# The linear recurrence of a two-layer model, computed in two stages by way of DRAM

## The chip, the cores and the metric

The kernel runs on one core of a Trainium2 chip. The metric is the device time of one execution in microseconds. Three executions of the kernel before took 2215.34, 2216.55 and 2222.05 us, median 2216.55.

## The reference

A model of two layers and one more block, 512 tokens of width 1024, all float32. The change lies in the first layer, the RWKV-7 time mix, with 32 heads of 64 features:

```python
r = xr @ w_in[0]; k = xk @ w_in[1]; v = xv @ w_in[2]; g = xg @ w_in[3]      # 1024 -> 2048 each
w_log = -softplus(-(w0 + tanh(xw @ w1) @ w2)) - 0.5
decay = exp(-exp(w_log));  a = sigmoid(a0 + (xa @ a1) @ a2)
kk = heads(k * k_k);  kk = kk / max(norm(kk), L2_EPS)
k = k * (1 + (a - 1) * k_a)
# per head and token t, state S of 64 x 64:
#   S = S * decay_t - (S kk_t)(a_t * kk_t)^T + v_t k_t^T ;  y_t = S r_t
y = head_group_norm(y, lnx_w, lnx_b)
bonus = sum(r * k * r_k, per head) * v
y = (y + bonus) * silu(g)
out = y @ w_out
```

Behind it come a short convolution layer and a block with attention, a long depthwise convolution and a gated feed-forward part. The change doesn't touch those.

## The kernel before

A float32 product of full width is made of three products in a rounded format: high x high, high x low, low x high ("dense" work; a k-group is one 128-row slice of the contraction, three matmuls of 128x512). The low part of a weight is the weight less its rounded copy. The products of the recurrence are plain float32.

`pre_phase` normalises, makes the token-shifted inputs and the value projection (to DRAM, `vD`). `scan_phase` then does everything up to the gate. It goes over 16 pairs of heads `j`. For one pair it makes the low-rank parts of decay and a (L617, L618), the k and r projections (16 k-groups, L701 to L703), and on VectorE the scaled keys `KB` and the vectors `ZR`. The tokens are cut into 8 chunks of 64. For all chunks of the pair, `gram` (L837) makes the 128x128 products of `KB` and `ZR`, which are masked (L845); `N` (L870) is the strictly triangular part, whose inverse `X` is found by 31 steps of one multiply and one subtract on VectorE (L923, L931) for the 32x32 diagonal blocks, and by two rounds of small products (L975) for the rest.

Then the 8 chunks follow one another. In each, TensorE makes `wy` from masked gram blocks and values (L1024) and from the state (L1033); ScalarE copies it, negated, to `Wn` (L1041); TensorE multiplies by the inverse (`U`, L1055); VectorE scales and copies `U` beside the values (L1063); TensorE makes the state's increment (`Sp`, L1072) and VectorE adds it to the decayed state (L1083, L1081 in the first chunk). The outputs get their last term from L1092. Each pair ends in a group norm: mean (L1160), 8 squared sums on ScalarE (L1168), a power on GpSimd (L1176), 8 scalings on ScalarE, then gain, bias, a transpose (L1197), and a store to `yD`.

After the pairs come 16 gate tiles: 8 k-groups each (L1283 to L1285), silu (L1291) into an SBUF tile, and a multiply by the stored y (L1299). `post_phase` begins with the output projection, for which `prep` splits those tiles in two parts.

The order of instructions on all five engines in this stage is written out by a planner, `list_schedule`. It takes the operations with their costs, priorities, dependences and buffer counts and, on a model of the engines, always starts the earliest one. In its model TensorE costs twice as much when too little work came shortly before, and a dense k-group is moved ahead when the recent share of work falls below `DENSITY`. Projections run `LAG` = 3 pairs ahead of the recurrence, and `pace` ties them to its links.

Of the kernel before, what the change touches and what calls it, by code (L numbers as in the profile page):

```python
# [25 lines left out]
C = 64  # L26
# [126 lines left out]
def two_block_kernel(ctx, tc, A, out):  # L153
# [100 lines left out]
    yD = dram.tile([DI, T], F32, tag="yD", name="yD")  # L254

    with ExitStack() as rk_ctx:
        hid = rk_ctx.enter_context(tc.tile_pool(name="hid", bufs=1))
        pd = rk_ctx.enter_context(tc.tile_pool(name="pd", bufs=2, space=PSUM))
        sgs, sconst, ahead = [], {}, {}
# [24 lines left out]
def pre_phase(nc, tc, A, E):  # L284
# [3 lines left out]
    vD, xgD, sconst, ahead = (E[k] for k in ("vD", "xgD", "sconst", "ahead"))  # L288

    def ht(shape, name, dt=F32):  # L290
        return hid.tile(shape, dt, tag=name, name=name)

    hidw, hida = ht([P, T], "hidw", F32R), ht([P, T], "hida", F32R)
    with ExitStack() as s:
# [213 lines left out]
        pack("pkB", ["b_conv_branch_2", "conv_dw_b_2", "conv_ln_g_2", "conv_ln_b_2"], hp, ps8, ahead["sp"])  # L508
# [7 lines left out]
        gmask = sconst["gmask"] = ht([P, 2 * P], "gmask")  # L516
        for b in (0, 64):
            for i in range(4):
                op = ALU.is_gt if i in (1, 2) else ALU.is_ge
                nc.gpsimd.affine_select(out=gmask[b:b + 64, 64 * i:64 * i + 64], in_=ones[b:b + 64, 0:64],  # L520
                                        pattern=[[1, 64]], compare_op=op, fill=0.0, base=0, channel_multiplier=-1)
        reset = sconst["reset"] = ht([P, NC, C + 1], "reset")
        nc.gpsimd.memset(reset, 1.0)
        nc.gpsimd.memset(reset[:, :, 0:1], 0.0)
        hind = sconst["hind"] = ht([P, 2], "hind")
        nc.gpsimd.memset(hind, 0.0)
        nc.gpsimd.memset(hind[0:64, 0:1], 1.0)
        nc.gpsimd.memset(hind[64:128, 1:2], 1.0)
# [9 lines left out]
        xone = sconst["xone"] = ht([P, 8, 32], "xone")  # L538
# [14 lines left out]
def scan_phase(nc, tc, A, E):  # L553
    col, cols, ident, ones, mhalf = (E[k] for k in ("col", "cols", "ident", "ones", "mhalf"))
    xr, xk, vD, xgD, yD, rc = (E[k] for k in ("xr", "xk", "vD", "xgD", "yD", "rc"))
    hidw, hida, wraw, whl, pd, kept = (E[k] for k in ("hidw", "hida", "wraw", "whl", "pd", "hid"))
    heads = [slice(0, 64), slice(64, 128)]
    with ExitStack() as s:
        sc = s.enter_context(tc.tile_pool(name="sc", bufs=1))
        pm = s.enter_context(tc.tile_pool(name="pm", bufs=3, space=PSUM))  # L560
        pc = s.enter_context(tc.tile_pool(name="pc", bufs=1, space=PSUM))

        def st(shape, name, bufs=1, dt=F32):
            return sc.tile(shape, dt, tag=name, name=name, bufs=bufs)
# [23 lines left out]
        def done_ahead():  # L588
            pass
# [7 lines left out]
        def build(j):  # L597
# [8 lines left out]
            if j == 0:  # L606
                S.update(E["ahead"])
# [1348 lines left out]
```

## Time and profile before

| | |
|---|---|
| median of three runs | 2216.55 us |
| profiled execution | 2209.47 us |
| its span, first to last instruction | 2207.8 us |
| PE / DVE / ACT / POOL busy in the span | 94 / 53 / 41 / 37 % |
| mean granted TensorE clock | 0.967 of full |
| HBM read / written | 175.80 / 14.68 MB |

PE is TensorE, DVE VectorE, ACT ScalarE, POOL GpSimd, SP SyncE (it issues the transfers). "L701" is line 701 of the kernel. Durations of PE instructions overlap in a pipeline, so the distance from one start to the next tells what one costs, not its duration. A float32 product of the recurrence appears in the timeline as two instructions (x4 stands for two products). "PEclk" is the granted clock as a share of the full one. In brackets stands how long an engine was idle before an instruction and what released it.

### The profile page before, as it was taken

To read this page: it belongs to the slowest core of one execution; us is meant where nothing else is said; L and a number is where in the kernel's file an instruction comes from. 1 tells how busy PE (TensorE), PEld (TensorE's weight loads), DVE (VectorE), ACT (ScalarE), POOL (GpSimd) and SP (SyncE) were. 2 spreads that over 40 slices of the span, in tenths; PEclk is the share of its full clock that TensorE was granted. 3 is DMA by queue.
4 is the path that set the end of the run, shared out by engine and by line. 5 is a ranking of instruction groups with operands and counts; after the bars stand their busy time and mean duration, and the time that the engine had idled before them with its cause. 6 is when DMAs were issued, how large, how long until landed. Compare 5 with 4: busy or idle time off the path is not lost.

```text
span 2207.8 us, 33093 instructions
## 1 busy us (share of the span) xinstructions
PE 2076.1 (94%) x12644; PEld 1600.6 (72%) x12644; DVE 1172.2 (53%) x2758; ACT 895.2 (41%) x1829; POOL 818.3 (37%) x710
## 2 busy tenths in 40 slices
PE   7998889889988999999999999999699999999998
PEld 5776666666666667788888888787466788888886
DVE  7959898888988762223333321379654253111101
ACT  5433465565555454323222222333476443222221
POOL 4220010110011233636555554665233366544442
PEclk9989999989898999999999999999799999999999
DMA  4341121121213233423333333333111242333321
GB/s 157 111 131 56 39 61 57 49 68 40 62 53 94 80 90 112 162 77 105 96 96 95 96 96 115 104 107 95 38 39 53 78 137 86 96 96 96 105 96 67
DMA packets 271607, 192.63 MB, mean 87 GB/s; under 512 B 12696, under 2 KB 238296, under 8 KB 271448
## 3 DMA queue, kind: packets, MB, share of 16 engines
q1 hardware_dynamic: 271448, 190.51, 28.4%
q8 instruction: 99, 1.62, 0.3%
q14 instruction: 60, 0.49, 0.1%
HBM read 175.80 MB, written 14.68 MB: 86 GB/s over the span
## 4 chain that ended last, share of the span: by engine, by line
PE 73%; DVE 16%; ACT 5%; issue 3%; POOL 2%; DMA 2%; SPq 0%; DVEq 0%; POOLq 0%; ACTq 0%
PE b L86 11%; PE b L85 11%; PE b L87 11%; PE b L120 5%; PE b L121 5%; PE b L119 5%; DVE conv L1730 4%; PE ps_d L701 3%; PE ps_d L703 2%; PE ps_d L702 2%; PE U L1055 2%; PE ps_g L1283 2%; DVE xtmp L923 2%; DVE X L931 1%; PE wy L1033 1%
## 5 line engine op out<-in xcount | busy, mean ns | idle before, releaser
L73 POOL TENSOR_TENSOR wl<-wr,wh 128x512 fp32r<-128x512 f32 (+1 forms) x463 | 639.8, 1404 | 602.2 <-ACT wh L65 596.2
L65 ACT CAST wh<-wr 128x1024 fp32r<-128x1024 f32 (+1 forms) x241 | 245.4, 1020 | 721.6 <-PE b L86 463.5
L87 PE MATMUL b<-s,wl 128*128 128x512 f32 x1024 | 404.7, 395 | 0.0
L86 PE MATMUL b<-s,wh 128*128 128x512 f32 x1024 | 404.4, 395 | 0.0
L85 PE MATMUL b<-s,wh 128*128 128x512 f32 x1024 | 403.4, 394 | 0.0
L85 PEld LDWEIGHTS b<-s,wh 128*128 128x128 f32 x1024 | 192.8, 188 | 47.2 <-issue 1.5
L86 PEld LDWEIGHTS b<-s,wh 128*128 128x128 f32 x1024 | 192.9, 188 | 46.0 <-issue 1.4
L87 PEld LDWEIGHTS b<-s,wl 128*128 128x128 f32 x1024 | 193.0, 188 | 43.6 <-issue 0.8
L1730 DVE SCALAR_TENSOR_TENSOR conv<-up,pkC,conv 128x512 f32<-128x512 f32 x120 | 117.0, 1040 | 0.4
L120 PE MATMUL b<-wl,s 128*128 128x512 f32 x288 | 113.9, 395 | 1.1 <-POOL wl L73 1.1
L923 DVE TENSOR_TENSOR xtmp<-dn,X 128x60 f32<-128x60 f32 (+24 forms) x496 | 109.1, 220 | 9.0
L119 PE MATMUL b<-wh,s 128*128 128x512 f32 x288 | 111.9, 396 | 1.2 <-ACT s L176 1.2
L121 PE MATMUL b<-wh,s 128*128 128x512 f32 x288 | 112.8, 395 | 0.0
L931 DVE TENSOR_TENSOR X<-X,xtmp 128x60 f32<-128x60 f32 (+24 forms) x496 | 106.3, 214 | 8.9
L628 POOL MEMSET sg<- 128x8 f32 x16 | 1.8, 116 | 283.8 <-ACT inv L658 168.5
L1849 DVE TENSOR_TENSOR a<-sg,b 128x512 f32<-128x512 f32 x22 | 15.1, 687 | 171.0 <-PE b L87 163.2
L1047 ACT ACTIVATE Sd<-St,pcl 128x64 f32<-128x64 f32 x96 | 33.1, 345 | 141.1 <-DVE St L1083 107.8
L1670 DVE TENSOR_TENSOR cu<-b,us 128x512 f32<-128x512 f32 x16 | 11.1, 692 | 126.1 <-PE b L87 120.5
L1055 PEld LDWEIGHTS U<-Wn,X 64*64 64x64 f32 x512 | 40.0, 136 | 51.0 <-issue 23.3
L1033 PE MATMUL wy<-St,ZR 64*64 64x64 f32 x672 | 56.6, 246 | 10.6 <-DVE St L1081 4.6
L701 PE MATMUL ps_d<-xk,wh 128*128 128x512 f32 x128 | 66.3, 518 | 0.0
L1055 PE MATMUL U<-Wn,X 64*64 64x64 f32 x512 | 57.8, 234 | 8.7 <-ACT Wn L1041 8.5
(347 smaller groups left out, 4435.7 us busy)
## 6 DMA issues: line engine op xcount, KB each, us to landing
wr<-in_b_w_in SPq DMA_DIRECT2D x64, 512.0 KB, 4.1
wr<-in_a_w_in SPq DMA_DIRECT2D x56, 512.0 KB, 3.9
wr<-in_w_ffn_up SPq DMA_DIRECT2D x44, 512.0 KB, 3.8
wr<-in_w_in SPq DMA_DIRECT2D x36, 512.0 KB, 3.8
wr<-in_w_ffn_down SPq DMA_DIRECT2D x22, 512.0 KB, 3.3
wr<-in_a_w_out SPq DMA_DIRECT2D x16, 512.0 KB, 3.5
wr<-in_b_w_out SPq DMA_DIRECT2D x16, 512.0 KB, 3.3
vD<-vst SPq DMA_DIRECT2D x16, 256.0 KB, 2.4
```

The costliest lines, as they stand in the source:

```text
L65: copy = self.nc.scalar.copy(out=hi[:, :n], in_=raw[:, :n])
L73: eng.tensor_tensor(out=lo[:, sl], in0=raw[:, sl], in1=hi[:, sl].bitcast(F32), op=ALU.subtract)
L85: nc.tensor.matmul(ps, wh[:, k, :], xh[k], start=k == 0, stop=False)
L86: nc.tensor.matmul(ps, wh[:, k, :], xl[k], start=False, stop=False)
L87: nc.tensor.matmul(ps, wl[:, k, :], xh[k], start=False, stop=k == nk - 1)
L119: nc.tensor.matmul(pss[t], th, wh[:, k, :], start=s, stop=False)
L120: nc.tensor.matmul(pss[t], th, wl[:, k, :], start=False, stop=False)
L121: nc.tensor.matmul(pss[t], tl, wh[:, k, :], start=False, stop=e)
L701: nc.tensor.matmul(ps, wh[:, k, :], x[0][:, k, :], start=k == 0, stop=False)
L923: nc.vector.tensor_tensor(out=S["xtmp"][:, c:, 0:p], in0=S["dn"][:, p:p + 1, 0:p].to_broadcast([P, w, p]), in1=S["X32"][:, c:, p:p + 1].to ...
L1055: nc.tensor.matmul(S["U"][qp, hd, :], S["X"][qp, hd, c // 2, :], S["Wn"][qp, hd, :], start=True, stop=True, skip_group_check=True)
L1730: nc.vector.scalar_tensor_tensor(out=conv[:, i, :], in0=up[:, i, tap:tap + T], scalar=col("conv_dw_w_2", tap * 4 + i), in1=conv[:, i, :], ...
```

## The change

The stage is cut in two. `chunk_phase` goes over all 16 pairs and makes projections, `KB`, `ZR` and `N`; it stores them to DRAM (512, 512 and 256 KB a pair). The two heads' sums of squares, which were 8 small products and small VectorE operations, become one 128x512 float32 product with a block matrix of ones (`ss_mm`), and the reciprocal runs on all 512 columns. The bonus sums stay in SBUF for all pairs.

`scan_phase` then goes over 8 groups `q` of two pairs each. It loads the group's tiles, makes gram products in 64x64 quadrants (64 of 128 columns a group), the masks, the transposes and the inverse for both pairs in one set of 62 VectorE instructions, and runs the 8 chunks for both pairs together: four quadrant or half products where there were two. The old state is added into the same accumulator by a product with the identity (`s_old`) instead of a scaled copy. One of the two `u_out` copies goes to ScalarE. The group norm works on two pairs in two halves, and gain and bias are applied behind the transpose.

The gate's tiles now run between the links of the recurrence (`when` ties tile i to a chunk). Their low parts move from GpSimd to VectorE. silu's result goes to DRAM (`sgD`), and `prep` of the output projection loads y and the gate back and multiplies them. The planner loses the model of the clock and gets a cost, `SWITCH`, for a change between full, half and quadrant tiles.

```diff
+    sgD = dram.tile([DI, T], F32, tag="sgD", name="sgD")
+    kbD, zrD, nD = ([dram.tile([P, w], F32, tag=f"{n}{j}", name=f"{n}{j}") for j in range(KI)]
+                    for n, w in (("kbD", 1024), ("zrD", 1024), ("nD", T)))
...
         xr, xk, hidw, hida = pre_phase(nc, tc, A, locals())
+        kz = rk_ctx.enter_context(tc.tile_pool(name="kz", bufs=1))
+        for name, shape in (("sums", [P, KI // 2, NC, 2]), ("pcl", [P, KI // 2, 2, NC])):
+            sconst[name] = kz.tile(shape, F32, tag=name, name=name)
+        chunk_phase(nc, tc, A, locals())
+        first_ctx.close()
         scan_phase(nc, tc, A, locals())
...
+def own(p, c):
+
+    return (c + p) % 2
...
+            def ss_mm():
+                S["ss"] = pl.tile([P, T], F32, tag="l", name="ps_ss")
+                nc.tensor.matmul(S["ss"], hones, S["ksq"].rearrange("p c s -> p (c s)"), start=True, stop=True)
+            op("PE", 0.95, ss_mm, j + 0.7, K("ss"), [K("ksq")], ["ksq"], ["l"], mode="w")
+
+            def rn():
+                S["rn"] = st([P, NC, C], "rn")
+                nc.vector.tensor_scalar(out=S["rn"], in0=chunks(S["ss"]), scalar1=1e-24, scalar2=2.0, op0=ALU.max,
+                                        op1=ALU.mult)
+                nc.vector.reciprocal(out=S["rn"], in_=S["rn"])
...
+            def n_mm():
+                ps = S["ps_n"] = pn.tile([P, 2, NC, C], F32, tag="n", name="ps_n")
+                kb, zr = (S[n].rearrange("p (c s f) -> p c s f", c=NC, s=2) for n in ("KB", "ZR"))
+                for c in range(NC):
+                    u = own(p, c)
+                    for hd in range(2):
+                        nc.tensor.matmul(ps[HEADS[u], hd, c // 2, :], kb[HEADS[hd], c, u, :], zr[HEADS[hd], c, u, :],
+                                         start=True, stop=True, skip_group_check=True)
...
+            def store(src, dst):
+                def go():
+                    t = S[src]
+                    nc.sync.dma_start(out=dst[j], in_=t if src != "N" else t.rearrange("p hd cp f -> p (hd cp f)"))
+                return go
+            op("SP", 0.2, store("KB", kbD), j + 0.9, K("st_kb"), [K("kb_b")], ["KB"], dma=2.5)
+            op("SP", 0.2, store("ZR", zrD), j + 1.2, K("st_zr"), [K("zr_r")], ["ZR"], dma=2.5)
+            op("SP", 0.2, store("N", nD), j + 1.5, K("st_n"), [K("n_mask")], ["N"], dma=1.3)
...
+            def ld(tag, src, p, bufs):
+                def go():
+                    S[tag, p] = kz.tile([P, 1024], F32, tag=tag, name=tag, bufs=bufs)
+                    nc.sync.dma_start(out=S[tag, p], in_=src[2 * q + p])
+                return go
...
+            def gram(p, b):
+                def go():
+                    ps = [pm.tile([P, 4, 2, C], F32, tag="m", name=f"ps_g{hd}") for hd in range(2)]
+                    S["gps", p, b] = ps
+                    kb, zr = chunked(S["KB", p]), chunked(S["ZR", p])
+                    for c in range(4 * b, 4 * b + 4):
+                        for slot in range(2):
+                            for hd in range(2):
+                                nc.tensor.matmul(ps[hd][HEADS[slot], c % 4, :, :], kb[HEADS[hd], c, slot, :],
+                                                 zr[HEADS[hd], c, :, :], start=True, stop=True, skip_group_check=True)
...
+            def ld_n():
+                S["N"] = st([P, 2, 2, NT, C], "N", 2)
+                for p in range(2):
+                    nc.sync.dma_start(out=S["N"][:, p].rearrange("p hd cp f -> p (hd cp f)"), in_=nD[2 * q + p])
...
+            def x_mul(i):
+                def go():
+                    if i == 31:
+                        S["xtmp"] = st([P, 2, 80], "xtmp")
+                    w, c = 8 - i // 4, i // 4
+                    nc.vector.tensor_tensor(out=tmp(i),
+                                            in0=S["dn"][:, :, i:i + 1, 0:i].to_broadcast([P, 2, w, i]),
+                                            in1=S["X32"][:, :, c:, i:i + 1].to_broadcast([P, 2, w, i]), op=ALU.mult)
+                return go
...
+            def mm(out, lhs, rhs, start=False):
+                nc.tensor.matmul(out, lhs, rhs, start=start, stop=True, skip_group_check=True)
+
+            def each(c):
+                for hd in range(2):
+                    for p in range(2):
+                        yield hd, p, HEADS[own(p, c)], HEADS[1 - own(p, c)]
...
+            def z_state(c, y):
+                def go():
+                    for hd, p, u, v in each(c):
+                        i, pa = (1 - own(p, c), v) if y else (own(p, c), u)
+                        mm(wy(pa, hd, c, y), chunked(S["ZR", p])[HEADS[hd], c, i, :], S["St", c - 1][HEADS[hd], p, :])
...
             def u_mm(c):
                 def go():
...
+                    S["us"] = pc.tile([P, 4, C], F32, tag="us", name="us")
+                    for hd, p, u, v in each(c):
+                        mm(S["us"][u, hd, :], S["X"][u, p, hd, c // 2, :], S["Wn"][u, hd, :], hd == 0)
...
+            def s_old(c):
+                def go():
+                    for hp in HEADS:
+                        mm(S["us"][hp, 2:4, :], ident[:, hp], S["St", c - 1])
+                return go
...
+            def u_out(c, p):
+                def go():
+                    u = HEADS[own(p, c)]
+                    (nc.scalar.copy if p else nc.vector.tensor_copy)(out=S["VU", p][u, c, :, :], in_=S["us"][u, 0:2, :])
...
+            def s_add(c):
+                def go():
+                    for p in range(2):
+                        for hp, hd in zip(HEADS, range(2)):
+                            mm(S["us"][hp, 2 + p, :], S["KBT", p][:, c, hp], S["VU", p][:, c, hd, :])
...
+                    S["St", c] = st([P, 2, C], "St", 2)
+                    nc.vector.tensor_tensor(out=S["St", c], in0=S["us"][:, 2:4, :],
+                                            in1=pcl[:, q, :, c:c + 1].to_broadcast([P, 2, C]), op=ALU.mult)
...
+                def sg_store():
+                    nc.sync.dma_start(out=sgD[i * P:(i + 1) * P, :], in_=S["sg"])
...
+                p0 = 0.2 + i / 2
+                at = max(0.0, (i - 1) * Q / (KI - 1))
+                when = [(int(at), "u_out", int((at % 1) * 8), 0)] if i else []
...
+                    op("PE", 0.69, dense(k), p0 + k / 16, K("dense", k),
+                       [K("w_lo", k // 4), ("g", "xg_lo", k)] + ([K("dense", k - 1)] if k else when),
+                       ["wh", "wl"] + (["d"] if k else []), [] if k else ["d"], mode="w")
...
+SWITCH = 0.2
...
-                pri = o["pri"]
-                if e == "PE" and o["key"][1] == "dense" and density(t0) < DENSITY:
-                    pri -= 1000
-                k = (t0, pri, o["i"])
+                k = (t0, o["pri"] + (0.02 if o["mode"] != mode else 0.0), o["i"])
...
-                a = q + 1e-9
+            if o["mode"] != mode:
+                cost += SWITCH
+            mode = o["mode"]
...
             for i in (2 * c, 2 * c + 1):
-                copy = split(y2[0][i], y2[1][i], sgs[i // KD][:, i % KD, :])
-                if i == 0:
-                    M.hold = partial(after, prev=copy)
-            if c == 1:
-                M.hold = None
+                y, g = (ep.tile([P, T], F32, tag=n, name=n, bufs=3) for n in ("yl", "gl"))
+                for t, src in ((y, yD), (g, sgD)):
+                    nc.sync.dma_start(out=t, in_=src[i * P:(i + 1) * P, :])
+                nc.vector.tensor_tensor(out=y, in0=y, in1=g, op=ALU.mult)
+                split(y2[0][i], y2[1][i], y)
```

TensorE, one chunk of the recurrence before, with the k projection of a later pair between (`wy`, `U`, `Sp` are the accumulators named above; L1197 is the transpose of a finished pair):

```order
L1033 MATMUL wy<-St,ZR_1168 64x64 x2
L1197 MATMUL yt<-ident,yc 128x128 x4
L701 MATMUL ps_d_5852<-xk_397,wh 128x512
L702 MATMUL ps_d_5852<-xk_398,wh 128x512
L703 MATMUL ps_d_5852<-xk_397,wl 128x512
L1055 MATMUL U<-Wn,X_1172 64x64 x2
L1033 MATMUL wy<-St,ZR_1168 64x64 x2
L701 MATMUL ps_d_5852<-xk_397,wh 128x512
L702 MATMUL ps_d_5852<-xk_398,wh 128x512
L703 MATMUL ps_d_5852<-xk_397,wl 128x512
L1072 MATMUL Sp<-VU,KBT 64x64 x2
L1092 MATMUL wy<-VU,G_4854 64x64
```

A k-group of the projection stands between any two links, and each link has two products of one pair.

TensorE, one chunk of the recurrence after, with gate tiles between (`us` holds U and the new state; `us<-St,ident` is `s_old`, `us<-VU,KBT` `s_add`):

```order
L1121 MATMUL us<-Wn,X_4018 64x64 x4
L1121 MATMUL us<-St,ident 64x128 x2
L1392 MATMUL ps_g<-xg_hi,wh 128x512
L1393 MATMUL ps_g<-xg_lo,wh 128x512
L1394 MATMUL ps_g<-xg_hi,wl 128x512
L1392 MATMUL ps_g<-xg_hi,wh 128x512
L1393 MATMUL ps_g<-xg_lo,wh 128x512
L1394 MATMUL ps_g<-xg_hi,wl 128x512
L1121 MATMUL us<-VU,KBT 64x64 x4
L1121 MATMUL wy<-VU,g_3578 64x64 x4
L1086 MATMUL ps_f<-XT,N 64x32 x32
L1121 MATMUL wy<-St,ZR 64x64 x8
```

Each link has four or eight products, of two pairs, and the round of 32 products for the next group's inverse (L1086) stands in the chain. In other chunks no k-group stands between two links.

SyncE, after, around the end of the recurrence (`yo` is a group's finished y; `yl` and `gl` are what the output projection loads; `V` the values for the bonus):

```order
L928 DMA V<-vD 64x4x128 x4
L1310 DMA yD<-yo 128x512 x2
L1402 DMA sgD<-sgt 128x512
L60 DMA wr<-in_a_w_out 128x2x512 x4
L1310 DMA yD<-yo 128x512 x2
L1689 DMA yl<-yD 128x512
L1689 DMA gl<-sgD 128x512
L1689 DMA yl<-yD 128x512
L1689 DMA gl<-sgD 128x512
L1689 DMA yl<-yD 128x512
```

All loads of y for the output projection stand behind the last store of y, where before they were made for the gate's multiply, a pair at a time, and the output projection read SBUF.

## Rows read from the trace of the kernel before

**Rows 1.** Timeline of PE: start, duration, engine, line, operation; edges of the stage.
```profile
138.66 0.40 PE L701 MATMUL ps_d<-xk,wh 128*128 128x512 f32 x1
...
881.68 0.50 PE L119 MATMUL b<-wh,s 128*128 128x512 f32 x1 [1.19 <-ACT s L176]
```

**Rows 2.** Windows: length, busy (count) of PE, PEld, DVE, ACT, POOL; PEclk, DMA, GB/s.
```profile
155.00:720.00 565.00, 504.90 (x5031) 358.41 (x5030) 490.40 (x1687) 304.19 (x786) 51.76 (x92) 0.92 0.20 58
720.00:852.00 132.00, 125.60 (x1102) 86.21 (x1100) 83.13 (x241) 62.89 (x167) 35.83 (x26) 0.96 0.32 92
852.00:885.00 33.00, 31.81 (x140) 25.18 (x140) 9.72 (x14) 18.32 (x43) 16.74 (x11) 1.00 0.38 122
1750.00:1800.00 50.00, 50.00 (x217) 39.92 (x216) 27.21 (x31) 18.97 (x31) 31.97 (x27) 1.00 0.56 181
```

**Rows 3.** Instructions of tile wy: duration min/median/max in ns, first and last start.
```profile
L1041 ACT ACTIVATE Wn<-wy x128: 253/272/275, 211.8 to 850.0; 64x128 f32<-64x128 f32 x128
```

**Rows 4.** Timeline of PE, one step of the recurrence beside the gate.
```profile
845.19 0.40 PE L1285 MATMUL ps_g<-xg_hi,wl 128*128 128x512 f32 x1
...
845.78 0.50 PE L1283 MATMUL ps_g<-xg_hi,wh 128*128 128x512 f32 x1
...
846.35 0.39 PE L1285 MATMUL ps_g<-xg_hi,wl 128*128 128x512 f32 x1
...
847.04 0.50 PE L1283 MATMUL ps_g<-xg_hi,wh 128*128 128x512 f32 x1
...
847.61 0.39 PE L1285 MATMUL ps_g<-xg_hi,wl 128*128 128x512 f32 x1
...
848.65 0.50 PE L1283 MATMUL ps_g<-xg_hi,wh 128*128 128x512 f32 x1
```

**Rows 5.** Timeline of PE, one small product group behind another of other shape.
```profile
509.16 0.40 PE L1024 MATMUL wy<-VU,G 128*64 128x64 f32 x4
509.56 0.33 PE L1033 MATMUL wy<-St,wr 64*64 64x64 f32 x4
```

**Rows 6.** Timeline of PE, a burst of small products and two dense products, low clock.
```profile
401.03 1.07 PE L975 MATMUL ps_f<-XT,N 64*32 64x32 f32 x32 [3.79 <-DVE G L845]
...
408.56 0.63 PE L701 MATMUL ps_d<-xk,wh 128*128 128x512 f32 x1
...
408.99 0.63 PE L702 MATMUL ps_d<-xk,wh 128*128 128x512 f32 x1
```

**Rows 7.** Timeline of PE, four 128-column transposes.
```profile
865.86 0.63 PE L1197 MATMUL yt<-ident,yc 128*128 128x128 f32 x4
```

**Rows 8.** Groups of DVE by line, 138 to 740: count | busy, mean ns | idle.
```profile
L845 DVE TENSOR_TENSOR G<-ps_g,gmask 128x512 f32<-128x512 f32 x62 | 42.1, 682 | 5.1 <-PE ps_g L837 4.6
...
L1063 DVE TENSOR_TENSOR VU<-U,sums 64x128 f32<-64x128 f32 x105 | 30.1, 286 | 24.9 <-PE U L1055 23.1
...
L911 DVE STREAM_TRANSPOSE dn<-N 128x1024 f32<-128x1024 f32 x15 | 18.5, 1231 | 0.1
...
L637 DVE TENSOR_SCALAR sg<-sg 128x520 f32<-128x520 f32 x15 | 6.3, 420 | 0.0
...
L819 DVE RECIPROCAL sums<-sums 128x8 f32<-128x8 f32 x16 | 3.2, 203 | 0.6
...
L1161 DVE TENSOR_SCALAR mu<-mu 128x8 f32<-128x8 f32 x13 | 2.2, 171 | 0.5
```

**Rows 9.** Groups of DVE by line and shape, whole span.
```profile
L923 DVE TENSOR_TENSOR xtmp<-dn,X 128x28 f32<-128x28 f32 x32 | 5.7, 179 | 0.4
...
L923 DVE TENSOR_TENSOR xtmp<-dn,X 128x76 f32<-128x76 f32 x16 | 3.8, 240 | 0.5
```

**Rows 10.** Timeline of DVE, the last pair's group norm: mean and first step behind.
```profile
853.14 0.69 DVE L1160 TENSOR_REDUCE mu<-yc 128x8 f32<-128x512 f32 x1 [1.00 <-ACT yc L1154]
...
863.82 0.69 DVE L1189 TENSOR_TENSOR yc<-yc,lnw 128x512 f32<-128x512 f32 x1 [3.76 <-ACT yc L1181]
```

**Rows 11.** DMA issues: count, KB each, median us from issue to landing.
```profile
kap<-yD SPq DMA_DIRECT2D x8, 256.0 KB, 2.6
```

More of the change, by code (lines that the diff above doesn't have):

```diff
@@ new lines, with over, op, emit_ops @@
+HEADS = (slice(0, 64), slice(64, 128))
+def own(p, c):
+    return (c + p) % 2
+def over(t, n):
+    return t.rearrange("p (a f) -> p a f", a=1).to_broadcast([t.shape[0], n, t.shape[1]])
+class Ops(list):
+    def op(self, eng, cost, fn, pri, key, deps=(), use=(), new=(), dma=0.0, mode=None):
+        self.append(dict(eng=eng, cost=cost, fn=fn, pri=pri, key=key, deps=deps, use=use, new=new, dma=dma, mode=mode,
+                         j=key[0]))
+def emit_ops(nc, tc, ops, bufs):
+    ET = mybir.EngineType
+    order = list_schedule(ops, bufs)
+    with tc.manual_schedule(engines={ET.PE, ET.DVE, ET.Activation, ET.Pool, ET.SP}):
+        for o in order:
+            o["fn"]()
@@ L1209, in build @@
-            op("ACT", 0.48, yc(0), j - 9, K("yc", 0), [K("av", NC - 2)], [("wy", "chain", 0)], ["yc"])
-            op("ACT", 0.48, yc(1), j - 9, K("yc", 1), [K("av", NC - 1), K("yc", 0)], [("wy", "chain", 0), "yc"])
-            op("DVE", 0.8, mean, e, K("mean"), [K("yc", 0), K("yc", 1)], ["yc"], ["mu"])
-            for u in range(8):
-                op("ACT", 0.33, var(u), e, K("var", u), [K("var", u - 1) if u else K("mean")], ["yc", "mu"], [])
-            op("POOL", 2.13, gn, e, K("gn"), [K("var", 7)], ["mu"])
@@ new lines, in bonus, with go, turn @@
+            def bonus(b):
+                def go():
+                    v = heads_of("V", b)
+                    rk = sums[:, q, 4 * b:4 * b + 4, :].rearrange("p c (hd o) -> p (c hd) o", o=1)
+                    nc.vector.tensor_tensor(out=v, in0=v, in1=rk.to_broadcast([P, 8, C]), op=ALU.mult)
+                return go
+            def turn(b):
+                def go():
+                    for n in "VY":
+                        ps = S["t" + n, b] = pm.tile([P, T], F32, tag="m", name="t" + n)
+                        for i in range(4):
+                            nc.tensor.transpose(ps[:, i * P:(i + 1) * P], S[n][:, 4 * b + i, :, :], ident)
+                return go
@@ L1232, in ld_xg, with gate @@
+            for p in range(2):
+                op("SP", 0.2, y_store(p), e, K("y_store", p), [K("total", p, 0), K("total", p, 1)], ["yo"], dma=1.0)
+        xg = []
+        def gate():
             def ld_xg(k):
@@ L1330, in scan_phase @@
[L1330 to L1341 removed]
+        for q in range(Q):
+            build(q)
+        gate()
+        emit_ops(nc, tc, L, dict(KB=2, ZR=4, V=1, VU=4, m=4, G=4, KBT=4, N=2, dn=1, X32=1, xtmp=1, Xd=1, X64=2, XT=1, FT=1, wy=1,
+                                 Wn=2, us=1, St=2, Y=2, mu=2, yo=1, wr=2, wh=2, wl=2, d=1, sgt=2))
```

1043 lines of the change are left out of this document (469 added, 574 removed).

## The prediction

> **What bounds the kernel now.** I read the busy shares first, then the windows, then PE's timeline and DVE's groups in the recurrence. The stage that the change replaces runs on PE from the first k product to the first product of the output projection, 138.66 to 881.68 us, 743.0 us [rows 1]. The reader should see in the first window that no single engine sets its pace: PE is busy 89% of it and DVE 87%, at a granted clock of 0.92 [rows 2]. Each engine's instructions are in a written order, so a late DVE result stalls PE and the reverse. One recurrence step is marked by one Wn copy: 127 intervals from 211.8 to 850.0 us make 5.03 us a step, 40.2 us a pair of heads [rows 3]. What limits it in the end is the sum of PE work and of waits for DVE, not a transfer: 58 GB/s there [rows 2].
>
> **Prices on PE.** In the last window 217 products of 128x512 fill 50 us, 0.23 us each, at clock 1.00 [rows 2]. Beside the gate, a k-group ends 0.23 after 845.19; the next starts at 845.78, 0.36 later, with two 64x64 products between. From 846.35 the same gap holds four and is 0.46. So a 64x64 quadrant product costs 0.05, and leaving the dense work and coming back 0.26. From 847.61 the gap is 0.81 with six 128-row products: 0.09 each [rows 4]. A 64-row product group that follows two 128-row ones starts 0.40 behind them [rows 5] where the price of two is 0.18: a change of shape among the small products costs about 0.2 as well.
>
> Changing the shape therefore costs even without dense work between, and the changed order has 112 such places in the recurrence, 22 us. [...] If only entering and leaving the dense work cost something, the forecast would be 20 us lower.
>
> **Chunk stage (new).** Per pair PE has 52 dense products (48 and 4 low-rank), 11.9 us; the sum of squares as one 512-column float32 product, 0.7 (a 128-column float32 transpose takes 0.16 [rows 7], four of them 0.64); 16 quadrant products for N, 0.8; 8 sums, 0.7; three excursions, 0.8. That is 14.9. DVE has 13 full 128x512 operations at 0.68, 8.9; scan, scaling and small ones about 2.8 (the scan is priced as the equally wide transpose, 1.23) [rows 8]; and the new 512-wide RECIPROCAL. The trace shows only one of 8 columns, 203 ns. TENSOR_SCALAR takes 171 ns for 8 columns and 420 for 520, so 0.49 ns a column and 167 fixed; the reciprocal then has 36 ns for 8 columns, 4.5 ns each, 2.5 us for 512 [rows 8]. Its ends are 0.68 (like any other operation) and 4.9 (twice the slope, since 8 columns resolve it poorly); I take 2.5, nearest to its own row. DVE then has 14.2, with ends 12.4 and 16.6. Both engines lie close, so 15.5 a pair, 248 for 16 (238 to 268).
>
> [...]
>
> Stores add 1.25 MB a pair to 1 MB of weights: 145 GB/s, against 58 in the present recurrence and 181 in the busiest window [rows 2]. I cost them at nothing behind PE; at the 122 GB/s of the gate window [rows 2] they would take 18.4 a pair, 47 us in all.
>
> **Start of the recurrence (new, exposed).** The old kernel computes the first pairs' inverse beside projections. Now the two-pair group's N comes back from DRAM (2.6 for 256 KB [rows 11]), then two diagonal copies 1.2, two transposes 2.5 [rows 8], the inverse chain with the masks between 20, transposes, placement and two rounds of 32 products 7, hops 4: 38 (34 to 44). Nothing dense is free to run there but the first gate tile.
>
> **A group of two pairs, PE.** 88 quadrant products x 0.05 = 4.4; 92 of 128 rows x 0.09 = 8.3; 12 for the old state, twice as wide, 2.2; 64 gram products, 128 columns, 0.10 each, 6.4; 64 products for the inverse 2.9 (16 half as wide take 1.07 while dense products stand 0.43 apart, at about half clock [rows 6]: 0.033 each at full, 0.045 taken, 0.067 at most); 32 transposes x 0.16 [rows 7] = 5.1; 48 gate products 11.0; 13 excursions x 0.26 = 3.4; 14 changes of shape x 0.2 = 2.8. Sum 46.5.
>
> **A group, DVE.** 8 masks x 0.68 = 5.5, two transposes 2.5 [rows 8]. The inverse's 62 multiplies and subtracts run once for two pairs on twice the elements: 28 elements take 179 ns and 76 take 240 [rows 9], 1.27 ns an element and 143 fixed; the mean is 50 elements, so 0.21 becomes 0.27, 16.8 in all, where the old kernel pays 26 for two pairs. 15 chain copies x 0.286 = 4.3 [rows 8]; two gate tiles' low parts, which POOL made before, 2.7; group norm, bonus and totals 4.8; small transposes 1.6. Sum 38.2.
>
> **What a group takes.** By DVE's present share (87%), 38.2 gives 44; by PE's (89%), 46.5 gives 52. A step needs four hops, PE to ACT, to PE, to DVE and ACT, to PE, to DVE, and the old steps filled them with three k-groups of projections; the new order has about two, and gram and inverse products of the next group instead. I take 50 (43 to 62). Seven groups make 350; the last has no next group to prepare, 37.
>
> **End (exposed).** The last group norm takes 10.7 us from its mean to the end of its scaling [rows 10], which the old kernel covers with seven gate tiles. In the new order gate tiles are used up between the steps, and the loads of y behind it stand on SP's queue after the last store of y. 10.7, copy, transposes and totals 3, store and load back 5.2 (2.6 each [rows 11]), multiply, split and hops 3: 22 (17 to 27).
>
> **Sum.** 138.7 + 248 + 38 + 350 + 37 + 22 = 833.7 against 881.7: 48 us less. POOL's lighter queue and the gate's multiply, which moves behind the stage with the same count, add nothing: neither ends a chain. The profiled execution took 2209.5 us (span 2207.8), 7.1 below the median of 2216.55. The sum is made in its time, 2161.5, and the forecast in terms of the median is 2169 us.
>
> **Rivals.**
> (a) DVE's pace, with a cheap reciprocal: groups of 43 and chunks of 14.9. For it: halved instruction count in the inverse. Against: PE has more priced work than that. 7 x 7 + 10 = 59 more, 2110 us. Chance 0.22.
> (b) Slower: lockstep. Both pairs' chains wait in the same hops, and gram, transposes and inverse of the next group come on top instead of filling them. A step of 5.03 us [rows 3] grows by the doubled products, 1.2 to 6.2 us; eight make 50, and 12 of the other work remain: 62 a group, and 46 for the last. For it: in the first window PE already waits though dense work abounds. Against: the 4.0 us steps beside the gate, which hold three k-groups (845.78 less 0.26 and 848.65 bound most of one) [rows 4]. It decides from 57 a group on (50 + 48/7). 7 x 12 + 9 - 48 = +45: 2262 us. Chance 0.20.
> (c) No gain because something general slows: a granted clock of 0.85 instead of 0.92 in the recurrence, since dense products are rarer there (57 a group), or stores that bind the chunk stage at 122 GB/s. Either eats the 48: about 2217 us. Chance 0.10.
>
> **Chances and range.** The main case has 0.48, its own range 2125 to 2212. About 0.3%, 6.6 us, is what a measurement of this kernel tells from no change, so faster means under 2210. Faster: 0.46 of the main case, (a) 0.22 and 0.02 of (c), 0.70. Same: 0.02 of the main case and 0.06 of (c), 0.08. Slower: (b) 0.20 and the rest of (c), 0.22. The range reaches from a group at 42 with the cheap reciprocal, 2090, to most of (b), 2250.
>
> **What would show it.** Right: last dense projection near 387 us; Wn copies 6.2 us apart on average, 64 of them; PE over 85% busy between; a gap of some 35 us with little PE work after the chunk stage, and one of 20 before the output projection. RECIPROCAL of 512 columns at 2.5 us, the gram group at 0.10 a product. Wrong: chunk pairs further apart than 17 us, with DVE never idle (reciprocal) or SP's stores landing late (transfers); groups above 57 with PE waiting for DVE copies or for Wn (lockstep), or a PEclk below 0.85 in the recurrence; a first product of the output projection that does not wait for loads of y.

## The result and the profile after

Four executions of the changed kernel took 2158.09 to 2164.08 us, median 2161.62, against a median of 2215.95 us before: ratio 0.975, interval 0.9725 to 0.9774. One execution of a later kernel, gram_order, took 3023.13 us at a granted clock of 0.61 and is left out of its figures. The forecast was 2169, within 2090 to 2250. The stage got shorter by about what was forecast, but three of its four parts did not take the time that was worked out for them.

The profiled execution took 2158.09 us. PE's timeline (start, duration), the first projection and the first product of the output projection, answers to [rows 1]:

```profile
139.02 0.39 PE L726 MATMUL ps_d<-xk,wh 128*128 128x512 f32 x1
...
826.45 0.80 PE L119 MATMUL b<-wh,s 128*128 128x512 f32 x1 [8.86 <-ACT s L176]
```

The stage ends at 826.45 instead of 881.68, 55.2 us earlier. What follows it takes 1330.0 instead of 1326.1. The windows of its four parts, with the columns of [rows 2]: chunk stage, start of the recurrence, recurrence, end.

```profile
139.00:382.00 243.00, 237.79 (x1613) 173.58 (x1612) 225.78 (x314) 108.24 (x174) 1.56 (x14) 1.00 0.47 154
382.00:458.00 76.00, 35.19 (x489) 29.59 (x490) 44.33 (x119) 20.92 (x33) 4.46 (x9) 0.63 0.66 191
458.00:800.00 342.00, 316.55 (x5272) 237.29 (x5272) 236.88 (x719) 214.03 (x639) 48.05 (x73) 0.95 0.34 108
800.00:826.00 26.00, 4.13 (x24) 2.29 (x18) 2.69 (x6) 10.26 (x31) 6.96 (x7) 0.50 0.41 135
```

The chunk stage keeps PE 98% busy at a granted clock of 1.00, and the recurrence keeps it 93% busy at 0.95. Between and behind them PE is busy 46% and 16% of the time, at 0.63 and 0.50.

**Chunk stage: 243 where 248 was forecast.** DVE's group of the new reciprocal, in the form of [rows 8], and the last mask of N, which ends the stage:

```profile
L790 DVE RECIPROCAL rn<-rn 128x512 f32<-128x512 f32 x16 | 53.7, 3353 | 0.5
```
```profile
382.00 0.69 DVE L837 TENSOR_TENSOR N<-ps_n,gmask 128x512 f32<-128x512 f32 x1
```

The reciprocal takes 3.35 us, between the 2.5 taken and the 4.9 of the bound. With the 167 ns fixed cost of the prediction that is an estimated 6.2 ns a column. DVE is 93% busy, but PE is 98% busy and nearly sets the pace (no_recip below shows what the reciprocal adds).

**Start: 76 where 38 was forecast.** DVE's timeline from the last mask on, then PE's first product of U (in brackets the idle time before and what released it):

```profile
390.13 1.25 DVE L1017 STREAM_TRANSPOSE dn<-N 128x1024 f32<-128x1024 f32 x1 [6.73 <-ACT N L1009]
...
397.54 0.69 DVE L1354 TENSOR_TENSOR xg_lo<-xg_lo,xg_hi 128x512 fp32r<-128x512 f32 x1 [6.16 <-ACT xg_hi L1349]
...
405.87 0.69 DVE L1383 TENSOR_TENSOR wl<-wr,wh 128x512 fp32r<-128x512 f32 x1 [5.12 <-ACT wh L1376]
...
422.48 0.69 DVE L964 TENSOR_TENSOR g<-ps_g,gmask 128x512 f32<-128x512 f32 x1 [5.16 <-PE ps_g L957]
```
```profile
457.86 1.30 PE L1121 MATMUL us<-Wn,X 64*64 64x64 f32 x8 [0.74 <-ACT X L1104]
```

With a second transpose right behind the one at 390.13, the inverse could have begun at about 392.6 (an estimate from that one's 1.25); it begins at 411.20, for in DVE's written order the low parts of the gate's input (`xg_lo`), of the gate's weights (`wl`) and the masks of the next group stand ahead of it or among its steps, and each of these waits: 6.2, 5.1 and 5.2 us. What `xg_lo` waits for is a load:

```profile
L1344 SPq DMA_DIRECT2D xg_lo<-xgD x8: 319/421/929, 388.2 to 396.2; - x8
...
DMA to landing us min/median/max: 6.2/8.3/8.6
```

A 256 KB load landed in 2.6 us in [rows 11]; here the median of eight is 8.3, among the loads of both groups' tiles and of the first weights.

**Recurrence: 342 where 387 was forecast.** The `Wn` copies, in the form of [rows 3], and PE's timeline in one stretch:

```profile
L1149 ACT ACTIVATE Wn<-wy x64: 253/278/304, 413.3 to 799.4; 128x128 f32<-128x128 f32 x64
```
```profile
586.69 0.40 PE L1394 MATMUL ps_g<-xg_hi,wl 128*128 128x512 f32 x1
587.01 0.45 PE L1121 MATMUL us<-Wn,X 64*64 64x64 f32 x8
587.39 0.50 PE L1392 MATMUL ps_g<-xg_hi,wh 128*128 128x512 f32 x1
...
588.29 0.45 PE L1121 MATMUL wy<-VU,g 128*64 128x64 f32 x8
588.67 2.06 PE L1086 MATMUL ps_h<-X,FT 64*64 64x32 f32 x64
590.65 1.15 PE L1121 MATMUL wy<-VU,g 128*64 128x64 f32 x32
...
592.53 0.60 PE L1285 MATMUL tV<-ident,V 128*128 128x128 f32 x4
592.97 0.60 PE L1285 MATMUL tY<-ident,Y 128*128 128x128 f32 x4
...
594.96 0.45 PE L1121 MATMUL us<-VU,KBT 128*64 128x64 f32 x8
595.25 0.40 PE L1121 MATMUL wy<-VU,g 128*64 128x64 f32 x8
595.58 1.53 PE L957 MATMUL ps_g<-ZR,KB 64*64 64x128 f32 x32
...
600.02 1.10 PE L957 MATMUL ps_g<-ZR,KB 64*64 64x128 f32 x32
601.05 0.45 PE L1121 MATMUL us<-VU,KBT 128*64 128x64 f32 x8
...
766.33 0.45 PE L1121 MATMUL us<-Wn,X 64*64 64x64 f32 x8
```

The first copy stands 44.6 us ahead of the first U, so the steps are counted by U. From the first U at 457.9 to the last at 800.0 are 342.1 us: 63 steps of 5.43. The last group's first U stands at 766.33, so that the seven groups with another behind them took 44.1 each (50 were forecast) and the last 33.7 to its last U (37). Starts give the prices: 4 products of 128 rows 0.29 (594.96 to 595.25), 0.07 each; 16 gram products 1.03 (600.02 to 601.05), 0.064; four transposes 0.44; 32 products of the inverse 1.98. A change of shape costs 0.04 to 0.09 (0.33 from 595.25 and 0.38 from 588.29, against 0.29). An excursion from dense work with four quadrant products, 586.69 to 587.39, is 0.70, as in [rows 4] (0.23 and 0.46).

**End: 26.5 where 22 was forecast.** The timeline of ACT, SP and DVE behind the last U:

```profile
805.95 1.99 ACT L65 CAST wh<-wr 128x1024 fp32r<-128x1024 f32 x2 [3.75 <-DMA wr<-in_a_w_out]
...
807.85 0.34 ACT L1254 ACTIVATE scr<-Y,mu 128x64 f32<-128x64 f32 x1
...
818.68 0.81 SPq L1310 DMA_DIRECT2D yD<-yo  x2
821.58 0.32 SPq L1689 DMA_DIRECT2D yl<-yD  x1
...
825.01 0.69 DVE L1690 TENSOR_TENSOR yl<-yl,gl 128x512 f32<-128x512 f32 x1 [5.91 <-DMA gl<-sgD]
```

The last mean is ready at 803.1. The variance starts at 807.85, behind two weight casts of the output projection, one of which waits for its load. From there on it is the forecast chain, 18.6 us to the first product.

### The profile page after: what moved, and what is told of

The parts are those of the page before. It is cut to its first block, busy times and chain, and to the rows that moved or that the text cites. A ratio compares the mean times of both kernels' runs of the same rounds, so it can differ in the third digit from the quotient of the medians.

```text
span 2156.4 us, 34526 instructions
## 1 busy us (share of the span) xinstructions
PE 1997.7 (93%) x13700; PEld 1567.2 (73%) x13700; DVE 1109.4 (51%) x1975; ACT 857.6 (40%) x1701; POOL 769.3 (36%) x684
## 4 chain that ended last, share of the span: by engine, by line
PE 69%; DVE 18%; ACT 4%; issue 4%; DMA 2%; POOL 2%; SPq 0%; DVEq 0%; POOLq 0%; ACTq 0%
PE b L86 11%; PE b L85 11%; PE b L87 11%; PE b L120 5%; PE b L121 5%; PE b L119 5%; DVE conv L1780 4%; PE us L1121 3%; DVE rn L790 2%; PE wy L1121 2%; PE ps_g L1392 2%; DVE wl L716 2%; POOL wl L73 1%; PE ps_g L1394 1%; PE ps_g L1393 1%
## 5 line engine op out<-in xcount | busy, mean ns | idle before, releaser
L119 PEld LDWEIGHTS b<-wh,s 128*128 128x128 f32 x288 | 54.7, 190 | 25.5 <-ACT s L176 12.6
L1035 DVE TENSOR_TENSOR xtmp<-dn,X 128x120 f32<-128x120 f32 (+24 forms) x248 | 65.0, 262 | 15.9 <-ACT X L1023 9.7
L1043 DVE TENSOR_TENSOR X<-X,xtmp 128x120 f32<-128x120 f32 (+24 forms) x248 | 65.3, 263 | 6.8
L1392 PE MATMUL ps_g<-xg_hi,wh 128*128 128x512 f32 x128 | 63.8, 499 | 3.1 <-ACT wh L1376 3.1
L1121 PE MATMUL wy<-VU,g 128*64 128x64 f32 x1024 | 53.9, 239 | 11.4 <-ACT Wn L1149 6.9
L120 PEld LDWEIGHTS b<-wl,s 128*128 128x128 f32 x288 | 54.8, 190 | 12.8
```

Source lines behind the costliest of these rows:

```text
L119: nc.tensor.matmul(pss[t], th, wh[:, k, :], start=s, stop=False)
L120: nc.tensor.matmul(pss[t], th, wl[:, k, :], start=False, stop=False)
L1043: nc.vector.tensor_tensor(out=X, in0=X, in1=tmp(i), op=ALU.subtract)
L1121: nc.tensor.matmul(out, lhs, rhs, start=start, stop=True, skip_group_check=True)
L1392: nc.tensor.matmul(S["ps"], wh[:, k, :], xg[0][:, k, :], start=k == 0, stop=False)
```

## The experiments

Medians in us; ratio to the kernel before, run beside each (its medians there are 2213.3 to 2217.6); "start" runs from the last mask of N to the first U, "recurrence" from the first U to the last, "end" from there to the first product of the output projection (profiled execution of each). In gate_end the gate stands behind the last U, so it has no end in this sense.

| kernel | median | ratio, interval | start | recurrence | end |
|---|---|---|---|---|---|
| changed kernel | 2161.62 | 0.975 (0.9725, 0.9774) | 75.9 | 342.1 | 26.5 |
| late_gate | 2149.05 | 0.9689 (0.9661, 0.9717) | 55.4 | 347.8 | 26.3 |
| act_hold | 2157.72 | 0.9733 (0.9702, 0.9763) | 76.1 | 345.1 | 24.3 |
| gate_end | 2272.26 | 1.0248 (1.0215, 1.0281) | 73.2 | 365.6 | - |
| x_per_pair | 2152.56 | 0.971 (0.9681, 0.9739) | 74.9 | 344.0 | 24.7 |
| gram_order | 2191.52 | 0.989 (0.9856, 0.9923) | 80.4 | 373.0 | 24.5 |
| gate_two | 2148.54 | 0.9694 (0.9661, 0.9728) | 75.8 | 337.9 | 24.6 |
| no_recip | 2148.39 | 0.9697 (0.9664, 0.9729) | 76.6 | 342.8 | 24.8 |
| combo2 | 2147.03 | 0.9696 (0.9664, 0.9729) | 52.5 | 358.9 | 26.4 |
| u_out_dve | 2160.27 | 0.9765 (0.9748, 0.9783) | 77.7 | 338.4 | 25.9 |
| combo5 | 2139.53 | 0.9664 (0.9647, 0.968) | 51.8 | 347.1 | 24.1 |

### late_gate: what the start waits for

```diff
-op("SP", 0.2, ld_xg(k), -0.9, ("g", "ld_xg", k), [], dma=0.9)
+op("SP", 0.2, ld_xg(k), -0.9, ("g", "ld_xg", k), [(0, "x_sub", 31)], dma=0.9)
-op("DVE", 0.69, xg_lo(k), 0.3, ("g", "xg_lo", k), [("g", "xg_hi", k)])
+op("DVE", 0.69, xg_lo(k), 0.3, ("g", "xg_lo", k), [("g", "xg_hi", k), (0, "x_sub", 1)])
... (ld_w, w_lo alike; gram of group 1 behind (0, "h_mm"))
```

> Only the planner's input is changed: the gate's inputs and first weights load and are split after the first group's inverse on DVE, and the second group's masks come behind it. Theory: the first U product stands 75 us behind the chunk stage because the inverse's 62 instructions queue on DVE behind operations that wait for gate loads and between masks of the next group. Then the first U product (457.9 us before) comes at about 430 and the kernel takes about 27 us less, 2135. Rival: the start is set by the amount of DMA and PE work, which is only moved into the first group; the U product may come earlier, but the total stays within 6 of 2162.

The start shrank by 20.5, the recurrence grew by 5.7, the median fell by 12.6. DVE's first and last step of the first inverse (in the changed kernel the first is at 411.20):

```profile
400.76 0.21 DVE L1036 TENSOR_TENSOR xtmp<-dn,X 128x62 f32<-128x62 f32 x1
...
419.04 0.19 DVE L1044 TENSOR_TENSOR X<-X,xtmp 128x16 f32<-128x16 f32 x1
```

The 62 instructions run unbroken in 18.4 us. So the order of DVE's queue and of the loads, which this edit moves together, was worth 20 of the 38 us that the forecast missed. The first U came at 438.07 where 430 was expected: the size expected was too large.

### act_hold: what the end waits for

```diff
+        M.hold = partial(after, prev=LAST[0])     # LAST: the last scaling of the group norm
         ws = out_proj(A["a_w_out"][0], y2, KI,
```

> Only ScalarE's order at the end of the recurrence is changed: the casts of the output projection's first weights stand behind the last scaling of the group norm. Theory: the squared sums waited 4.6 us behind two casts that waited for their weights' DMA, on the path to the output projection, so the total falls by 4 to 5 us, 2157. Rival: the weights' low parts are then late and the first product of the output projection waits for them instead: 2162 or more.

The end shrank by 2.2 us; one cast still stands ahead. The variance starts 4.2 us behind the last U instead of 7.9, but part of that is lost again, for two casts now stand before the last copies of y:

```profile
816.31 1.98 ACT L65 CAST wh<-wr 128x1024 fp32r<-128x1024 f32 x2
818.19 1.01 ACT L1302 ACTIVATE yo<-tY,pkB 128x256 f32<-128x256 f32 x2
```

The medians differ by 3.9 us and the intervals overlap: by time alone this stays unclear.

### gate_end: dense work between the links

```diff
-                when = [(int(at), "u_out", int((at % 1) * 8), 0)] if i else []
+                when = [(Q - 1, "u_out", NC - 1, 0)]
```

> All gate tiles are tied to the last chunk of the last group, so that no dense work stands between the links. Theory that PE's summed work sets a group's 43.4 us: a group loses 11.0 of dense products and 3 of excursions and takes 30 to 33; 16 tiles add 88 behind, of which they cover about 18 of the last group norm: total 2140 to 2150. Rival, that the chain's hops set it and dense work fills waits: a group keeps 38 or more, and the total is 2161.6 - 8 x 5 + 88 - 18 = 2190 or more.

The recurrence does not get shorter without the gate's 88 us of products (384 x 0.23); it takes 23.5 longer, 46.4 for 8 of its 63 steps against 43.4. The rest of the 111 us is the gate itself, now between the last U at 820.9 and the first product of the output projection at 945.6. Windows of the recurrence, columns as above:

```profile
440.00:820.00 380.00, 301.18 (x5024) 246.79 (x5024) 230.72 (x722) 193.49 (x610) 42.86 (x69) 0.63 0.23 70
```

PE has no dense product there, is busy 79% and is granted 0.63 instead of 0.95. The same small products last longer (the median instruction of U 311 ns instead of 218), and from the first U to the last PE stands idle 71 us instead of 25. Both lengthen the chain; their shares aren't separated. The gate tiles are nearly free where they stand: with them the recurrence took 342.1 at a granted clock of 0.95, without them 365.6.

### gate_two: a third of the dense work less

```diff
-                        nc.tensor.matmul(S["ps"], wh[:, k, :], xg[1][:, k, :], start=False, stop=False)
```

> Leaves out one of the gate's three products (low part of the input), a third of the dense work between the links: 16 products or 3.7 us a group. Theory that a group is PE's summed work: 40 a group instead of 43.4, total 2130 to 2140. Rival, that the dense products fill waits of the chain and hold the clock up: groups within 1 us, total within 8 of 2162, or more where the granted clock falls.

29 us of products less shorten the recurrence by 4.2, far from the sum of PE's work; the total, 2148.5, lies between what the two theories gave. Of the same 60 us stretch, the changed kernel and then this one:

```profile
640.00:700.00 60.00, 54.38 (x940) 40.95 (x932) 49.11 (x152) 38.46 (x114) 8.21 (x13) 0.97 0.37 117
```
```profile
640.00:700.00 60.00, 54.26 (x858) 40.05 (x856) 45.81 (x149) 33.70 (x107) 6.90 (x12) 0.83 0.35 108
```

In this stretch PE is as busy as before with fewer products, at a lower granted clock; over the whole recurrence it is busy 91% at 0.90. How much of the 25 us went into the clock and how much into hops that the products had covered isn't separated.

### gram_order: the price of quadrant products

```diff
-                    for c in range(4 * b, 4 * b + 4):
-                        for slot in range(2):
-                            for hd in range(2):
+                    for slot in range(2):
+                        for hd in range(2):
+                            for c in range(4 * b, 4 * b + 4):
```

> Only the order of the 16 gram products of one half is changed: those of one quadrant of TensorE stand one behind the other, where before neighbours lay in four different quadrants. Theory: the small products were cheaper than priced (gram 0.066 us instead of 0.10) because four quadrants work at once. Then a burst of 16 goes from 1.05 us to about 3, the gram products of a group from 4.2 to 12 us, and a group from 43.4 to about 50; total 2200 to 2225. Rival, that the issue of instructions sets the price, whatever the quadrant: within 6 of 2162.

The same 16 products, now four in a row in one quadrant:

```profile
614.44 2.56 PE L957 MATMUL ps_g<-ZR,KB 64*64 64x128 f32 x32
```

About 2.1 to 2.5 us a burst instead of 1.03, and the recurrence grows by 30.9. So a product costs 0.13 to 0.16 where four in a row share a quadrant and 0.064 where neighbours alternate. 24 of the 32 bursts lie between the first U and the last (the first two groups' come earlier); at 1.1 to 1.4 more they are 26 to 34 us, and all of it appears in the time: extra PE work is paid here, while less dense work gains next to nothing. The total stayed below the 2200 to 2225 expected, since a burst had been put at 3 us.

### x_per_pair: does one wide instruction save time?

```diff
-nc.vector.tensor_tensor(out=tmp(i), in0=S["dn"][:, :, i:i + 1, 0:i]..., in1=S["X32"][:, :, c:, i:i + 1]..., op=ALU.mult)
+for j in range(2):
+    nc.vector.tensor_tensor(out=tmp(i)[:, j], in0=S["dn"][:, j, i:i + 1, 0:i]..., in1=S["X32"][:, j, c:, i:i + 1]..., op=ALU.mult)
... (the subtract alike)
```

> One part undone: each of the 62 steps of the inverse is two instructions of one pair each, as before the change, in the same order. DVE gets 62 x (2 x 0.21 - 0.26) = 10 us more a group, 34.7 to 44.7. Theory: DVE had 20% of slack in a group of 43.4 and binds now: 46 to 48 a group, and 4 more in the start, total 2185 to 2205. Rival, that the DVE work is hidden beside PE: within 6 of 2162.

Refuted: with twice the instructions the kernel isn't slower (nor clearly faster: the intervals overlap). DVE's timeline, the step of 120 elements in the changed kernel, then the two halves of 60 here:

```profile
437.88 0.28 DVE L1035 TENSOR_TENSOR xtmp<-dn,X 128x120 f32<-128x120 f32 x1
438.19 0.28 DVE L1043 TENSOR_TENSOR X<-X,xtmp 128x120 f32<-128x120 f32 x1
438.51 0.30 DVE L1035 TENSOR_TENSOR xtmp<-dn,X 128x132 f32<-128x132 f32 x1
```
```profile
508.98 0.34 DVE L1036 TENSOR_TENSOR xtmp<-dn,X 128x60 f32<-128x60 f32 x2
509.24 0.34 DVE L1045 TENSOR_TENSOR X<-X,xtmp 128x60 f32<-128x60 f32 x2
509.50 0.37 DVE L1036 TENSOR_TENSOR xtmp<-dn,X 128x76 f32<-128x76 f32 x2
```

A step takes 0.63 us in the wide form and 0.52 in the narrow one. Here a wide instruction, which needs the one before it, starts 0.03 behind its end; the two halves don't need each other and overlap by 0.08 (0.21 each, the mean of 48, and 0.34 together).

### no_recip: the reciprocal

```diff
-nc.vector.tensor_scalar(out=S["rn"], in0=chunks(S["ss"]), scalar1=1e-24, scalar2=2.0, op0=ALU.max, op1=ALU.mult)
-nc.vector.reciprocal(out=S["rn"], in_=S["rn"])
+nc.vector.tensor_scalar(out=S["rn"], in0=chunks(S["ss"]), scalar1=0.0, scalar2=0.006, op0=ALU.mult, op1=ALU.add)
```

> Leaves out the reciprocal of 512 columns (a constant takes its place as the keys' scale): 3.35 us a pair of DVE's 14.1 in the chunk stage, in which PE is busy 99% of the time. Theory: PE sets the stage, 15.0 us a pair, and only the last pair's tail becomes shorter: total 3 to 5 us less. Rival, that DVE sets it (94% busy): 16 x 1 to 3 us less, 2115 to 2145.

The masks of N in the changed kernel, then here:

```profile
L837 DVE TENSOR_TENSOR N<-ps_n,gmask x16: 672/676/692, 158.9 to 382.0; 128x512 f32<-128x512 f32 x16
```
```profile
L836 DVE TENSOR_TENSOR N<-ps_n,gmask x16: 681/692/692, 159.0 to 372.6; 128x512 f32<-128x512 f32 x16
```

The last mask comes at 372.6, 9.4 earlier: of 54 us of reciprocals, PE hides 44. The rest isn't a tail behind the last pair: over 15 intervals the pairs stand 14.24 us apart on average instead of 14.87, so DVE costs PE 0.6 in each. Neither expectation fits; the total, 2148.4, lies between them.

### u_out_dve: a copy on a second engine

```diff
-                    (nc.scalar.copy if p else nc.vector.tensor_copy)(out=S["VU", p][u, c, :, :], in_=S["us"][u, 0:2, :])
+                    nc.vector.tensor_copy(out=S["VU", p][u, c, :, :], in_=S["us"][u, 0:2, :])
... (the planner's engine for it alike)
```

> Edit: both copies of U beside the values (u_out) run on VectorE; in the changed kernel one runs on ScalarE. Question: what a hop of the recurrence is made of. Theory: the two copies read one accumulator and already run one behind the other (in the changed kernel ScalarE's starts at 605.42, VectorE's at 605.71, with VectorE put down as waiting for ScalarE), so the second engine saves nothing: recurrence 342 us as before within 5, total 2154 to 2168. Rival: the two copies overlap in part; then each of 64 chunks gets 0.25 us longer, 16 us in all, recurrence 358, total 2178.

Two copies in the changed kernel, on two engines, then here on one:

```profile
605.42 0.26 ACT L1168 COPY VU<-us 64x128 f32<-64x128 f32 x1 [1.38 <-PE us L1121]
605.71 0.28 DVE L1168 COPY VU<-us 64x128 f32<-64x128 f32 x1 [0.66 <-ACT VU L1168]
```
```profile
594.48 0.61 DVE L1168 COPY VU<-us 64x128 f32<-64x128 f32 x2
```

0.57 from first start to last end against 0.61: the second engine saves nothing, and the time is the same. Why they run one behind the other isn't shown; U in two accumulators wasn't tried.

### combo2 and combo5: the edits together

`combo2` is late_gate, act_hold and x_per_pair, the first group's masks behind the first step of the inverse, and the last two gate tiles behind the last chunk:

```diff
-                at = max(0.0, (i - 1) * Q / (KI - 1))
+                at = max(0.0, (i - 1) * Q / (KI - 3))
+                if i >= KI - 2:
+                    when = [(Q - 1, "u_out", NC - 1, 0)]
```

> Five edits together: gate inputs and the second group's masks behind the first inverse; the first group's masks behind it too; the inverse in one instruction for each pair; the output projection's weight casts behind the last scaling; the last two gate tiles behind the last chunk, where TensorE waits for the group norm. Theory of separate gaps: 2149 (first edit alone) less 6 (masks), 9 (inverse by pairs), 4 (casts) and 10 (two tiles, 11 us of PE work, moved into an idle stretch of 15): about 2120. Rival, that the gaps overlap or the last groups slow down for want of dense work: 2140 or more.

```profile
436.00:795.00 359.00, 327.46 (x5338) 250.37 (x5336) 251.11 (x1181) 215.40 (x641) 43.23 (x69) 0.90 0.34 105
```

The start gained 23 and the recurrence lost 17, at a clock of 0.90, and the end is no shorter. That the loss comes from the two tiles missing between the links isn't shown apart from the other edits. `combo5` is late_gate and act_hold with the tiles where they were and the wide inverse, and holds back more of what stood in the first inverse's way:

```diff
-K("w_lo", hf), [K("w_hi")] + ...
+K("w_lo", hf), [K("w_hi"), (0, "u_out", 0, 0)] + ...
-("g", "xg_lo", k), [("g", "xg_hi", k)])
+("g", "xg_lo", k), [("g", "xg_hi", k), (0, "xt")])
-[K("gram", p, b)], [("m", "gram", p, b), ("G", "gram", p, 0)])
+[K("gram", p, b)] + ([(0, "x_sub", 20)] if q == 0 else []), [("m", "gram", p, b), ("G", "gram", p, 0)])
```

> Edit: as late_gate, and besides the low parts of the gate's first tile and inputs wait until the first inverse is transposed (its input) or the first U is copied (its weights), the first group's masks until step 20 of the inverse, and the output projection's weight casts wait for the last scaling. Inverse as in the changed kernel, gate tiles spread as there. Theory (start and end are exposed and add up, 76 and 27 us): start 46 instead of 76, end 24, recurrence 348 as in late_gate, total 2140. Rival: the gate's first tile, ready later, leaves the first group without dense work, so that the recurrence grows by what the start gains and the total stays at 2147 to 2150, as with late_gate alone.

```profile
383.00:435.00 52.00, 22.27 (x354) 20.51 (x356) 32.70 (x88) 16.42 (x27) 4.46 (x9) 0.57 0.74 226
435.00:782.00 347.00, 324.26 (x5409) 243.33 (x5406) 248.60 (x751) 215.97 (x643) 43.15 (x69) 0.97 0.36 113
```

The total is as expected, 2139.5, the fastest kernel of this study, though the start took 51.8 where 46 was expected. Its start comes closest to what the step costs by itself. On ScalarE, copies for a later product (`KBT`) still stand ahead of the inverse's placement in X:

```profile
421.71 0.59 ACT L984 COPY KBT<-ps_t 128x512 f32<-128x512 f32 x1 [1.83 <-PE ps_t L977]
...
424.65 1.33 ACT L1078 ACTIVATE X<-Xd,rmask 128x512 f32<-128x512 f32 x2
```

The mask of N is at 383.15, the transpose of the loaded N at 391.87, the first step of the inverse at 394.27, its end at 419.0, the first U at 434.91: 8.7, 2.4, 24.7 with the masks between, and 15.9.

## Why the prediction was right

The total came out because two large errors cancel, which is luck; that the change pays, and that PE stays busy through the recurrence, was foreseen. By its steps, against the forecast end of the stage at 833.7 (measured 826.45):

- **Chunk stage, 248: 243.** PE nearly set the pace, as priced. The reciprocal was under-sized by 0.85 us, and 44 of 54 us of it lie behind PE (no_recip). The stores, at 154 GB/s with PE 98% busy, cost nothing that shows.
- **Start, 38: 76.** The step that failed is the sentence on the start as a chain of its own. Its terms as written add up to 37.3. It counted the chain and not what the changed order had put into DVE's queue and SP's at the same place. late_gate and combo5 recover 20.5 and 24.1 of the missing 38. The other 14 are in combo5's start: the store of N, which the forecast left out, with its load and copies (8.7 against 2.6 and 1.2), masks among the steps (24.7 against 20), and products and copies behind the inverse at a granted clock of 0.57 (15.9 against 7 and 4 of hops; 2.7 of it the `KBT` copies).
- **Groups, 387 for eight: 342.** The term that was mis-sized is PE's sum. With prices by starts, 92 products of 128 rows are 6.4 (8.3 taken), 64 gram products 4.1 (6.4), 32 transposes 3.5 (5.1), 64 products of the inverse 4.0 (2.9), 14 changes of shape 0.6 to 1.3 (2.8), the rest as forecast and not measured singly: 39.6 to 40.3 instead of 46.5. With the 3.5 us of waiting that were forecast, that is 43.1 to 43.8, and 44.1 was measured for a full group. The sum fits, but a group isn't only PE's sum: gate_two took 3.7 us of products from each and shortened it by about 0.5. Transposes had been priced by duration over count, 0.63 for four in [rows 7], where the starts of two such groups stand 0.44 apart here (592.53 and 592.97) and each lasts 0.60; shape changes by the one gap of 0.40 in [rows 5], which isn't repeated here. The 0.2 that the prediction read from its own row is not borne out among the small products: here it is 0.04 to 0.09.
- **What covers the hops.** The forecast took lockstep as the rival, for want of dense work. PE was 93% busy. gate_end shows what (b) and (c) warned of: without gate tiles between the links PE idles more (71 us instead of 25), its granted clock falls to 0.63, and 8 steps take 46.4 instead of 43.4. (b) itself did not happen: a group took 44.1, not 62. (a) named nearly the right time for a group, 43, for a wrong reason: DVE is busy 69% of the recurrence, and its halved instruction count saves nothing (x_per_pair). (c) did not happen: the clock was 0.95.
- **End, 22: 26.5.** ACT's queue held the variance back by 4.7 us behind weight casts. The rest is 3.2 to the mean and the 18.6 of the forecast chain with its loads of y behind the last store on SP. act_hold gets back 2.2 of the 4.7.
- **Behind the stage, 0: 3.9 us more.** PE waits 2.6 us (1.1 before) as the output projection goes on from its first product, for the rounded copies `s` of the loaded tiles, and its first products stand 0.43 us apart (826.45 to 830.0) at a granted clock of 0.50, as far as those in [rows 6], where it was 0.50 as well; not foreseen.

Against the forecast: -5 in the chunk stage (382.0 against 386.7), +38, -45, +4.5: 826.

Which part of the change brings the 55 us isn't shown singly. The wide inverse and the copy on ScalarE were undone and are worth nothing that shows; the gate tiles' place between the links is worth 111 us; two pairs in one chain and the quadrant products were not undone.

## What to carry to other kernels

When a stage is cut in two, price the seam by everything that the written order of each engine holds at that place, with the loads that all become ready there, and not by the chain alone; then hold back what the chain does not need (here the start went from 75.9 to 51.8 us, combo5). Take the price of small products from one start to the next, not from durations (four transposes: 0.44 against 0.60). Dense work that fills a chain of small steps is worth leaving there even if it could go elsewhere: here removing it lengthened the recurrence from 342.1 to 365.6 us (gate_end).

## What was not expected of the hardware

- 16 quadrant products of 64x128 took 1.03 us when neighbours lay in different quadrants (changed kernel) and 2.1 to 2.5 when four in a row shared one (gram_order).
- Two VectorE instructions of 60 elements that don't need each other took 0.26 us from their start to the next pair's (x_per_pair), one of 120 that the next needs 0.31 (changed kernel): a step of 0.52 against 0.63.
- RECIPROCAL of 512 columns took 3.35 us, the mean of 16, where an equally wide TENSOR_TENSOR took 0.68 (changed kernel).
- Without dense products between the links, PE was 79% busy and was granted 0.63 of its clock (gate_end); with them it was 93% busy and was granted 0.95 (changed kernel).
